# Second mixer of an encoder trunk: queries and keys projected with features on the partitions, rotated by block swaps, values projected apart

## The chip, the cores and the metric

The kernel runs on one core of one Trainium2 chip. The metric is the device time of one execution, in microseconds (us). The core has a matrix engine (TensorE, PE), a vector engine (VectorE, DVE), an activation engine (ScalarE, ACT), GpSimd (POOL) and a queue engine (SyncE, SP). Each works through its own instructions in order, and DMAs are issued from the queues of SP, POOL or ACT. SBUF is the on-chip memory with 128 partitions, PSUM the memory that TensorE writes.

## What is computed

The reference is a trunk of two layers over two groups of requests, one sequence of 256 tokens and one of 512, with 1024 features. Each layer is a token mixer and a feed-forward part, both between RMS norms. The change is in the second mixer, differential attention:

```python
def diff_attention(h, w_in, w_o, lq1, lk1, lq2, lk2, subln_g, lambda_init):
    b, s, _ = h.shape
    qkv = h @ w_in
    q, k, v = jnp.split(qkv, [B_QK_DIM, 2 * B_QK_DIM], axis=-1)
    q = q.reshape(b, s, 2 * B_HEADS, HEAD_DIM)
    k = k.reshape(b, s, 2 * B_HEADS, HEAD_DIM)
    v = v.reshape(b, s, B_HEADS, 2 * HEAD_DIM)
    cos, sin = rope_tables(s, HEAD_DIM)
    q = (apply_rope(q, cos, sin) * (HEAD_DIM ** -0.5)).reshape(b, s, B_HEADS, 2, HEAD_DIM)
    k = apply_rope(k, cos, sin).reshape(b, s, B_HEADS, 2, HEAD_DIM)
...
        sc = jnp.einsum('bqhcd,bkhcd->bhcqk', qi, k).astype(jnp.float32)
        p = jax.nn.softmax(sc, axis=-1)
        a = p[:, :, 0] - lam * p[:, :, 1]
        return jnp.einsum('bhqk,bkhe->bqhe', a.astype(v.dtype), v)
...
    o = rms_norm(o, subln_g) * (1.0 - lambda_init)
    return o.reshape(b, s, B_V_DIM) @ w_o
```

There are 8 heads. A head has two halves (c above) of 64 features each for queries and keys, and one value of 128. `apply_rope` splits 64 features into two blocks of 32, and each block needs the other one: x1·cos − x2·sin and x2·cos + x1·sin.

## The kernel before, in words

**Tiling.** The 768 tokens are 6 tiles of 128 (t = 0 to 5): tiles 0 and 1 are the sequence of 256, tiles 2 to 5 that of 512. Everything is float32. A product is made of three matmuls of a rounded type (F32R): each operand is the sum of a high and a low part (`hi`, `lo`), and `product_steps` (L315 to L317) adds hi·hi, hi·lo and lo·hi. With 1024 features in 8 blocks of 128, a product is 24 matmuls. `h_hi` and `h_lo` hold the normed tokens with features on the partitions, in two halves of three tiles.

**Weights.** SP loads weights in blocks (`wraw`), ACT casts the high part (L222) and DVE subtracts it for the low part (L223), ahead of their use, into a ring of buffers. `take` gets the next block, `free` lets the ring go on.

**The units of the second mixer.** `mixer_b` runs 48 units, head by head and tile by tile. A unit (`unit`) multiplies one tile of tokens (the stationary operand) with 384 columns of weights (the moving one): q, k and v of one head, into a PSUM bank `pqb`, with tokens on the partitions. Its `end` copies v (L787), rotates q and k on DVE (`rope`, L530 to L536; there the two blocks lie in the free dimension), and splits them into high and low parts `bsp` (L794 to L798). Scores need features on the partitions. So two units later, after four steps of the products, `turn` runs: three transposes of k on TensorE into `tkb` (L808), two of q into `tqb` (L810), an ACT copy to `kb` (L811) and a DVE copy to `qb` (L812).

**Attention.** For each head and tile there are three steps. `score`: four matmuls into two banks `bsc` (L828, L831), the row maximum (L834), a tiny negation (L835), exponentials with their sum on ACT (L837), and the combination of both halves on DVE (`rden`, `rho`, `be`: L842 to L847). `turn_e`: transposes of the probabilities into `tpa` (L859) and a copy `aT` on ACT (L861). `values`: matmuls into `pob` (L871), an ACT copy into `ob` (L875) and the sum of squares (L877). From head 6 on, POOL scales a row's heads by the sub-norm: `rstd_sub` (L360, its first step on ACT in L359), then `ob` times it (L884): heads 0 to 6 at head 6, head 7 at head 7.

**Order.** The program is written in the order in which these pieces are called, and each engine takes its own in an order close to it. `plan` and `last_plan` say after which step of a unit's products a piece of attention is called; one call of `advance` is the score of a tile, the transposes of the tile two calls before and the values of the tile three calls before. After the units comes the out projection of 2 × 6 units (`po`, 512 columns each); its operands are transposes of `ob` into `tp_o` (L407), with ACT and DVE making high and low parts (L414, L415). The list `run` interleaves its first three units with the last pieces of attention by hand. `gains(2)`, two vectors of 1024 spread over the partitions (`gpost`, `gpre`), is loaded ahead of the mixer and used by the out projection. The pool `xpool` has two buffers with the tag "x" of 4 KB a partition.

Of the kernel before, what the change touches and what calls it, by code (L numbers as in the profile page):

```python
# [46 lines left out]
def trunk(  # L47
# [7 lines left out]
    wb,  # L55
    wo,
# [6 lines left out]
    sin,  # L63
    yp,
# [113 lines left out]
    for h in range(8):  # L178
        for i in range(4):
            plain(wb[h, i], 768)  # L180
# [584 lines left out]
    def mixer_b(gp, g_next, first_steps, o):  # L765
        with ExitStack() as st:
            ap = st.enter_context(tc.tile_pool(name="bpool", bufs=1, side="right", reuse_waits="tile"))
            ssh = [ap.tile([P, 8], F32, name=f"ssh{t}") for t in range(NT)]
            kk, vv, q, wk = {}, {}, {}, {}
            pending = {}  # L770

            def unit(i):

                h, t = divmod(i, NT)
                first, n = seq_of(t)
                if t == 0:
                    wk[h] = column_blocks(take(4), HALF)
                    free(4)
                pm = bank(f"pqb_{i}")
                steps = product_steps(pm[:, :HALF], [(htile(t, k), wk[h][k]) for k in range(KT)])  # L780
                if t == NT - 1:
                    steps = releasing(steps, 4)

                def end():
                    if t == first:
                        vv[h, first] = ap.tile([P, n, P], F32, tag=f"v{first}", name=f"vb{h}_{first}", bufs=2)
                    nc.scalar.copy(out=vv[h, first][:, t - first], in_=pm[:, 256:384])  # L787
                    qk = ap.tile([P, 4, HD], F32, tag="qk", name=f"bqk{i}", bufs=2)
                    rope(ap, qk, pm[:, :256].rearrange("p (n d) -> p n d", d=HD), 4, t, f"b{i}")

                    sp = ap.tile([P, 5, 2, HD], F32R, tag="sp", name=f"bsp{i}", bufs=2)
                    s4 = sp.rearrange("p a b d -> p (a b) d")
                    k2 = qk[:, 2:4].rearrange("p c (o d) -> p c o d", o=1).broadcast_to([P, 2, 2, HD])
                    nc.scalar.copy(out=s4[:, 0:4:3], in_=qk[:, 0:2])  # L794
                    nc.scalar.copy(out=sp[:, 2:4], in_=k2)
                    nc.vector.tensor_tensor(
                        out=s4[:, 1:3], in0=qk[:, 0:2], in1=s4.bitcast(F32)[:, 0:4:3], op=ALU.subtract)
                    nc.vector.tensor_tensor(  # L798
                        out=sp[:, 4], in0=qk[:, 2:4], in1=sp.bitcast(F32)[:, 2:4, 0], op=ALU.subtract)

                    def turn():
                        if t == first:
                            kk[h, first] = ap.tile([P, 3, n * P], F32R, tag=f"k{first}", name=f"kb{h}_{first}")
                        q[i] = ap.tile([P, 2, P], F32R, tag="q", name=f"qb{i}", bufs=5)
                        tq, tk = ps.tile([P, 512], F32R, tag="ps", name=f"tqb{i}"), ps.tile([P, 512], F32R, tag="ps", name=f"tkb{i}")
                        at = slice((t - first) * P, (t - first + 1) * P)
                        for j in range(3):
                            nc.tensor.transpose(tk[:, j * P:(j + 1) * P], sp[:, 2 + j].rearrange("p a d -> p (a d)"), ident_r)  # L808
                        for j in range(2):
                            nc.tensor.transpose(tq[:, j * P:(j + 1) * P], sp[:, j].rearrange("p a d -> p (a d)"), ident_r)  # L810
                        nc.scalar.copy(out=kk[h, first][:, :, at], in_=tk.bitcast(F32)[:, :3 * P].rearrange("p (k n) -> p k n", k=3))  # L811
                        nc.vector.tensor_copy(out=q[i].rearrange("p h n -> p (h n)"), in_=tq.bitcast(F32)[:, :256])  # L812

                    pending[i] = turn

                return steps + [end]
# [3 lines left out]
            def score(i):  # L820
                h, t = divmod(i, NT)
                first, n = seq_of(t)
                den = small.tile([P, 2], F32, tag="den", name=f"bden{i}")
# [3 lines left out]
                for c in range(2):  # L827
                    nc.tensor.matmul(ss[c], q[i][:, c], kk[h, first][:, c], start=True, stop=False)  # L828

                for c, rows in enumerate((slice(0, HD), slice(HD, P))):  # L830
                    nc.tensor.matmul(ss[c], q[i][rows, c], kk[h, first][rows, 2], start=False, stop=True)  # L831
                for c, s in enumerate(ss):
                    mx = small.tile([P, 1], F32, tag="mx", name=f"bmx{i}_{c}")
                    nc.vector.tensor_reduce(out=mx, in_=s, axis=AX.X, op=ALU.max)  # L834
                    nc.vector.tensor_scalar(out=mx, in0=mx, scalar1=-HD ** -0.5, scalar2=None, op0=ALU.mult)  # L835
                    e = e2[:, c * 512:c * 512 + 512]
                    nc.scalar.activation(  # L837
# [25 lines left out]

            def values(i):
                h, t = divmod(i, NT)
                first, n = seq_of(t)
                _, rden = blocks.pop(i)
                aT = aTs.pop(i)
                po = bank(f"pob{i}")
# [35 lines left out]
            for i in range(8 * NT):  # L905
# [16 lines left out]
                for s in placed(att, at, fill):  # L922
                    s()
# [555 lines left out]
```

## Time and profile before

| what | value |
|---|---|
| median of three runs | 1689.34 us (1686.83, 1689.34, 1690.02) |
| span of the profiled execution, first to last instruction | 1686.6 us |
| profiled execution's own time | not listed apart; its span lies 0.2 us under the fastest run |
| mean granted TensorE clock | 0.997 |
| first and last start of a product of the second mixer (`pqb`) | 790.3 and 1106.6 us |
| DVE, ACT, POOL busy, of the span | 74%, 56%, 5% |
| moved by DMAs | 207.30 MB, 123 GB/s on average |

The profile lists busy time by engine. TensorE's matmuls are pipelined: a listed duration overlaps the next one, so a matmul's price in a full queue is the distance from its start to the next start. A row of groups reads: line, engine, operation, out<-in, shapes, count, then busy us and mean ns, then the idle time ahead of them and what ended it. Three numbers with slashes are the shortest, median and longest duration in ns.

### The profile page before, as it was taken

Reading aid. Unit: us, or ns where it says so; the run is one execution under the profiler, and the core shown is the slowest. Engines: PE = TensorE matmul, PEld = TensorE weight load, DVE = VectorE, ACT = ScalarE, POOL = GpSimd, SP = SyncE. Lnnn points to the kernel's source line nnn. Section 1 sums busy time; section 2 is a strip of 40 time slices with the busy share of each in tenths; the row PEclk is TensorE's granted clock in tenths of the full one; section 3 lists DMA queues with packets and bytes.
Section 4 is the critical chain, followed back from the end, with each engine's and each line's share of the span. In section 5 each row is a group of like instructions: output and inputs, shape, how many; then the busy total and the mean of one; then the engine's idle time right before and its main releaser. Section 6 shows DMA issues by size and latency. Waiting matters only on the chain. (4 is left out here: it accounts for less than half of the span.)

```text
span 1686.6 us, 25513 instructions
## 1 busy us (share of the span) xinstructions
PE 1659.1 (98%) x9483; PEld 1514.3 (90%) x9483; DVE 1251.3 (74%) x2488; ACT 949.7 (56%) x2158; POOL 81.7 (5%) x104
## 2 busy tenths in 40 slices
PE   7999999999999999999999999999899999999998
PEld 7888878899999998888999999988799999998887
DVE  7888766896766666988777676874997666666886
ACT  6777775654444444556566666674744444444553
POOL 1000001000000000001000000331000000000001
PEclk9999999999999999999999999999999999999999
DMA  6111014534333347666211111113444343336765
GB/s 212 39 38 48 14 38 150 175 134 140 109 125 99 128 139 250 230 235 205 83 39 38 38 38 38 48 51 113 170 138 141 108 141 108 128 114 226 249 222 176
DMA packets 62107, 207.30 MB, mean 123 GB/s; under 512 B 6752, under 2 KB 8928, under 8 KB 61728
## 3 DMA queue, kind: packets, MB, share of 16 engines
q1 hardware_dynamic: 55152, 175.15, 30.8%
q0 software_dynamic: 6688, 30.28, 5.6%
q8 instruction: 74, 1.21, 0.3%
q14 instruction: 49, 0.40, 0.1%
q10 hardware_dynamic: 144, 0.26, 0.0%
HBM read 162.80 MB, written 42.86 MB: 122 GB/s over the span
## 5 line engine op out<-in xcount | busy, mean ns | idle before, releaser
L223 DVE TENSOR_TENSOR wlo<-wraw,whi 128x1024 fp32r<-128x1024 f32 (+2 forms) x180 | 204.9, 1144 | 173.9 <-ACT whi L222 172.7
L222 ACT CAST whi<-wraw 128x1024 fp32r<-128x1024 f32 (+2 forms) x180 | 176.5, 986 | 117.4 <-PE py L316 58.9
L315 PE MATMUL py<-hhi,whi 128*128 128x384 f32 x464 | 155.4, 335 | 0.8 <-ACT u L976 0.8
L317 PE MATMUL py<-hhi,wlo 128*128 128x384 f32 x464 | 155.0, 334 | 0.0
L316 PE MATMUL py<-hlo,whi 128*128 128x384 f32 x464 | 155.0, 334 | 0.0
L315 PE MATMUL pqb<-whi,hhi 128*128 128x384 f32 x384 | 136.5, 356 | 0.0
L316 PE MATMUL pqb<-wlo,hhi 128*128 128x384 f32 x384 | 128.9, 336 | 0.0
L317 PE MATMUL pqb<-whi,hlo 128*128 128x384 f32 x384 | 128.8, 335 | 0.0
L303 ACT CAST hhi<-araw 128x768 fp32r<-128x768 f32 (+1 forms) x74 | 57.6, 783 | 94.6 <-DMA araw<-act 94.2
L317 PE MATMUL pv<-whi,hlo 128*128 128x512 f32 (+1 forms) x240 | 92.2, 384 | 0.4 <-DVE hlo L304 0.4
L315 PE MATMUL pv<-whi,hhi 128*128 128x512 f32 (+1 forms) x240 | 92.4, 385 | 0.0
L316 PE MATMUL pv<-wlo,hhi 128*128 128x512 f32 (+1 forms) x240 | 92.1, 384 | 0.0
L304 DVE TENSOR_TENSOR hlo<-araw,hhi 128x768 fp32r<-128x768 f32 (+1 forms) x74 | 65.2, 889 | 32.3 <-ACT hhi L303 32.1
L315 PEld LDWEIGHTS py<-hhi,whi 128*128 128x128 f32 x464 | 87.1, 188 | 1.7 <-ACT u L976 1.4
L316 PEld LDWEIGHTS py<-hlo,whi 128*128 128x128 f32 x464 | 87.1, 188 | 0.0
L317 PEld LDWEIGHTS py<-hhi,wlo 128*128 128x128 f32 x464 | 87.1, 188 | 0.0
L315 PE MATMUL po<-whi,hhi 128*128 128x512 f32 x192 | 77.9, 406 | 0.2 <-ACT hhi L303 0.2
L317 PE MATMUL po<-whi,hlo 128*128 128x512 f32 x192 | 75.4, 393 | 0.2 <-DVE hlo L304 0.2
L316 PE MATMUL po<-wlo,hhi 128*128 128x512 f32 x192 | 75.3, 392 | 0.0
L315 PEld LDWEIGHTS pqb<-whi,hhi 128*128 128x128 f32 x384 | 72.3, 188 | 2.0 <-issue 1.7
L315 PE MATMUL pqa<-whi,hhi 128*128 128x384 f32 x192 | 73.9, 385 | 0.0
L315 PE MATMUL px<-hhi,whi 128*128 128x384 f32 x208 | 70.8, 342 | 2.7 <-ACT hhi L303 2.7
(303 smaller groups left out, 4829.6 us busy)
## 6 DMA issues: line engine op xcount, KB each, us to landing
act<-st POOLq DMA_DIRECT2D x22, 1344.0 KB, 6.6
wraw<-in_wgu SPq DMA_DIRECT2D x56, 512.0 KB, 4.6
araw<-act SPq DMA_DIRECT2D x70, 384.0 KB, 4.0
y_wraw<-in_wgu SPq DMA_DIRECT2D x40, 512.0 KB, 3.6
wraw<-in_wd SPq DMA_DIRECT2D x40, 512.0 KB, 3.9
wraw<-in_wb SPq DMA_DIRECT2D x32, 384.0 KB, 3.2
xd<-x SPq DMA_DIRECT2D x18, 512.0 KB, 3.0
x<-xd SPq DMA_DIRECT2D x18, 512.0 KB, 4.1
```

The source lines that it names most:

```text
L222: state["raw_hi"] = nc.scalar.copy(out=hi, in_=src)
L223: state["raw_lo"] = nc.vector.tensor_tensor(out=lo, in0=src, in1=hi.bitcast(F32), op=ALU.subtract)
L303: state["hi"] = nc.scalar.copy(out=hi, in_=src)
L304: state["lo"] = nc.vector.tensor_tensor(out=lo, in0=src, in1=hi.bitcast(F32), op=ALU.subtract)
L315: nc.tensor.matmul(out, ah, bh, start=start and i == 0, stop=False, skip_group_check=more)
L316: nc.tensor.matmul(out, ah, bl, start=False, stop=False, skip_group_check=more)
L317: nc.tensor.matmul(out, al, bh, start=False, stop=stop and i == last, skip_group_check=more)
```

## The change

Queries and keys are no longer projected tile by tile. `rotated` makes a unit of one head's q or k for one half of the tokens (three tiles): the weights are the stationary operand and 384 tokens the moving one, so the result (`pqb` or `pkb`) has features on the partitions, as scores need them. The two blocks of 32 features that rotation combines now lie on different partitions. ACT copies the result to `x` (L834, with the scaling of q), four DMAs from POOL's queue write it with neighbouring blocks of 32 partitions swapped (L836), and DVE multiplies the copy (L838) and the swapped one (L839) with tables `rope_b` and adds them (L840). ACT casts the two halves of 64 features (L849). For q, DVE subtracts the high from the full values into the other half's partitions (L852). For k, two more DMAs from POOL's queue copy the high parts there (L855), and DVE makes the low parts (L856). There are 32 such units. Values are projected apart by `straight`, for groups of 2, 3 and 3 heads and tile by tile, 18 units. `b_fill` is the order of these 50 units.

The tables take the buffers of `gpost` and `gpre`, and the gains are loaded after the units. Pieces of attention stand at positions in a list `events`, counted in units; `run` is written anew and holds two score tiles of head 6 and all six of head 7, with three out-projection banks open at once. The sub-norm is applied at heads 3, 6 and 7 (heads 0 to 3, 4 to 6, and 7). The negation of the row maximum is done by the maximum itself, and the exponential no longer scales. Line numbers in this section are those of the changed program.

```diff
+def b_fill():
+
+    qk = lambda hs, halves, kinds: [(kind, h, i) for i in halves for h in hs for kind in kinds]
+    v = lambda g: [("v", g, t) for t in range(NT)]
+    out = qk((0,), (0,), "qk") + v(0) + qk((0,), (1,), "qk")
+    for h in range(1, 8):
+        out += qk((h,), (0, 1), "qk") if h == 7 else qk((h,), (0, 1), "q") + qk((h,), (0, 1), "k")
+        if h in (2, 5):
+            out += v(h // 2)
+    return out
...
+        if kind == "v":
+            for i in range(4 if V_HEADS[n] == 3 else 2):
+                w = 2 * HALF if V_HEADS[n] == 3 else D
+                plain(wbv[n, i, :, :w], w)
+        else:
+            plain(wb[n, "qk".index(kind)], D)
...
+            tab = []
+            for i, tag in enumerate(("gpost", "gpre")):
+                full = gpool.tile([P, D], F32, tag=tag, name=f"rope{i}")
+                nc.sync.dma_start(out=full[:, :2 * HALF], in_=rope_b[i])
+                tab.append(full[:, :2 * HALF].rearrange("p (h n) -> p h n", h=2))
...
+            def rotated(kind, h, half):
+
+                (whi, wlo), = held((kind, h), 1)
+                bk = bank(f"p{kind}b{h}_{half}")
+                pm = bk[:, :HALF]
+                steps = product_steps(pm, [
+                    (tuple(w[:, k * P:(k + 1) * P] for w in (whi, wlo)), (h_hi[half][:, k], h_lo[half][:, k]))
+                    for k in range(KT)])
...
+                def end():
+                    x = xpool.tile([P, 2, HALF], F32, tag="x", name=f"x{kind}{h}_{half}")
+                    s, r = x[:, 0], x[:, 1]
+                    nc.scalar.activation(out=s, in_=pm, func=AF.Copy, scale=HD ** -0.5 if kind == "q" else 1.0)
+                    for a in range(4):
+                        nc.gpsimd.dma_start(out=r[a * 32:a * 32 + 32], in_=s[(a ^ 1) * 32:(a ^ 1) * 32 + 32])
+                    z = ap.tile([P, HALF], F32, tag="z", name=f"z{kind}{h}_{half}", bufs=2)
+                    nc.vector.tensor_tensor(out=z, in0=s, in1=tab[0][:, half], op=ALU.mult)
+                    nc.vector.tensor_tensor(out=r, in0=r, in1=tab[1][:, half], op=ALU.mult)
+                    nc.vector.tensor_tensor(out=z, in0=z, in1=r, op=ALU.add)
+                    if kind == "q":
+                        d = q[h, half] = ap.tile([P, 2, HALF], F32R, tag="q", name=f"qb{h}_{half}", bufs=4)
+                        homes = (d[:, 0], d[:, 1])
+                    else:
+                        if half == 0:
+                            kk[h] = ap.tile([P, 3, 2 * HALF], F32R, tag="k", name=f"kb{h}", bufs=2)
+                        homes = (kk[h][:, 0, cols], kk[h][:, 1, cols])
+                    for rows, b in zip((up, down), homes):
+                        nc.scalar.copy(out=b[rows], in_=z[rows])
+                    if kind == "q":
+                        for rows, other, b in zip((up, down), (down, up), homes):
+                            nc.vector.tensor_tensor(out=b[other], in0=z[rows], in1=b[rows].bitcast(F32), op=ALU.subtract)
+                    else:
+                        for rows, other, b in zip((up, down), (down, up), homes):
+                            nc.gpsimd.dma_start(out=b[other], in_=b[rows])
+                            nc.vector.tensor_tensor(
+                                out=kk[h][rows, 2, cols], in0=z[rows], in1=b[rows].bitcast(F32), op=ALU.subtract)
+
...
+            def straight(g, t):
+                n = V_HEADS[g] * P
+                taken = held(("v", g), 4 if n == HALF else 2)
+                wide = [tuple(w[:, j * n:(j + 1) * n] for w in u) for u in taken for j in range(KT // len(taken))]
+                pm = bank(f"pvb{g}_{t}")[:, :n]
+                steps = product_steps(pm, [(htile(t, k), wide[k]) for k in range(KT)])
...
+                    vv[g, t] = ap.tile([P, n], F32, tag="v", name=f"vb{g}_{t}", bufs=9)
+                    nc.scalar.copy(out=vv[g, t], in_=pm)
...
                     mx = small.tile([P, 1], F32, tag="mx", name=f"bmx{i}_{c}")
-                    nc.vector.tensor_reduce(out=mx, in_=s, axis=AX.X, op=ALU.max)
-                    nc.vector.tensor_scalar(out=mx, in0=mx, scalar1=-HD ** -0.5, scalar2=None, op0=ALU.mult)
+                    nc.vector.tensor_reduce(out=mx, in_=s, axis=AX.X, op=ALU.max, negate=True)
                     e = e2[:, c * 512:c * 512 + 512]
-                    nc.scalar.activation(
-                        out=e[:, :n * P], in_=s, func=AF.Exp, bias=mx, scale=HD ** -0.5,
-                        accum_out=den[:, c:c + 1])
+                    nc.scalar.activation(out=e[:, :n * P], in_=s, func=AF.Exp, bias=mx, accum_out=den[:, c:c + 1])
...
-                if h >= 6:
-
-                    hs = slice(0, 7) if h == 6 else slice(7, 8)
+                if h in (3, 6, 7):
+
+                    hs = {3: slice(0, 4), 6: slice(4, 7), 7: slice(7, 8)}[h]
...
+            events = []
+
+            def spread(h, start, stop):
+                for t in range(NT):
+                    events.append((start + (stop - start) * t / NT, "s", h * NT + t))
+
+            for h, start, stop in (
+                    (0, 12, 16.7), (1, 16.7, 22.2), (2, 22.2, 28.8), (3, 29.6, 34.8), (4, 34.8, 40.3), (5, 40.3, 46)):
+                spread(h, start, stop)
+            events += [(47.9 + t / 2, "s", 6 * NT + t) for t in range(4)]
+            for n in range(2, len(events)):
+                events.append((events[n][0], "t", n - 2))
+            for n in range(3, 6 * NT + 4):
+                events.append((events[n][0], "v", n - 3))
+            kinds = {"s": score, "t": turn_e, "v": values}
+            events.sort(key=lambda e: e[0])
+
...
+            gp, g_next = gains()
...
+            run = S(6, 4) + early[0] + T(6, 2) + V(6, 1) + early[1] + out[0][:2] + S(6, 5) + T(6, 3) + V(6, 2) + out[0][2:4]
+            run += S(7, 0) + early[2] + T(6, 4) + V(6, 3) + out[1][:2] + S(7, 1) + T(6, 5) + V(6, 4) + out[1][2:4] + early[3]
+            run += S(7, 2) + T(7, 0) + V(6, 5) + out[2][:2] + S(7, 3) + T(7, 1) + V(7, 0) + out[2][2:4] + early[4]
+            run += S(7, 4) + T(7, 2) + V(7, 1) + late[0] + early[5] + out[0][4:6] + S(7, 5) + T(7, 3) + V(7, 2) + late[1]
+            run += out[0][6:] + T(7, 4) + V(7, 3) + late[2] + out[1][4:6] + T(7, 5) + V(7, 4) + out[1][6:] + late[3]
+            run += out[2][4:6] + V(7, 5) + out[2][6:]
```

The removed lines that are left out are in the functions shown above. The host lays out the weights anew (`wb` by head and kind with 1024 columns, `wbv` by group) and makes the tables `rope_b`.

**TensorE, between two score tiles.** In the names of before, `pqb_15` is the product of unit 15, `tkb13` and `tqb13` the transposes of unit 13, `bsc11` a score of unit 11. Before:

```order
L317 MATMUL pqb_15_9688<-whi141_9340,hlo1_114 128x384
L808 MATMUL tkb13_9703<-ident_r_86,bsp13_9584 128x128 x3
L810 MATMUL tqb13_9702<-ident_r_86,bsp13_9584 128x128 x2
L315 MATMUL pqb_15_9688<-whi142_9398,hhi1_112 128x384
L316 MATMUL pqb_15_9688<-wlo142_9399,hhi1_112 128x384
L317 MATMUL pqb_15_9688<-whi142_9398,hlo1_114 128x384
L828 MATMUL bsc11_0_9716<-kb1_2_9261,qb11_9527 128x512
L828 MATMUL bsc11_1_9717<-kb1_2_9261,qb11_9527 128x512
L831 MATMUL bsc11_0_9716<-kb1_2_9261,qb11_9527 128x512
L831 MATMUL bsc11_1_9717<-kb1_2_9261,qb11_9527 128x512
L859 MATMUL tpa9_9735<-ident_81,be9_9600 128x128 x4
```

Now, where the first score of head 3 (`bsc18`) follows q of head 4 (`pqb4_1`, its second half of the tokens):

```order
L347 MATMUL pqb4_1_10237<-hlo1_114,whi146_9862 128x384
L348 MATMUL pqb4_1_10237<-hhi1_112,wlo146_9863 128x384
L890 MATMUL bsc18_0_10258<-kb3_10109,qb3_0_9961 128x256
L890 MATMUL bsc18_1_10259<-kb3_10109,qb3_0_9961 128x256
L893 MATMUL bsc18_0_10258<-kb3_10109,qb3_0_9961 128x256
L893 MATMUL bsc18_1_10259<-kb3_10109,qb3_0_9961 128x256
L918 MATMUL tpa16_10275<-ident_81,be16_10059 128x128 x4
L931 MATMUL pob15_10282<-vb1_2_9685,aT15_10159 128x128
```

The transposes of k and q are gone; the scores read `kb3` and `qb3_0`, which DVE, ACT and POOL's DMAs have written.

**DVE, in the third head before and at k of the fourth head now.** Before (`bqk18` is the rotated q and k of unit 18, `be14` the probabilities of unit 14):

```order
L796 TENSOR_TENSOR bsp18_10033<-bqk18_10026,bsp18_10033 128x128
L798 TENSOR_TENSOR bsp18_10033<-bqk18_10026,bsp18_10033 128x128
L812 CAST qb17_10051<-tqb17_10052 128x256
L834 TENSOR_REDUCE bmx14_0_10075<-bsc14_0_10069 128x1
L834 TENSOR_REDUCE bmx14_1_10079<-bsc14_1_10070 128x1
L835 TENSOR_SCALAR bmx14_0_10075<-bmx14_0_10075 128x1
L835 TENSOR_SCALAR bmx14_1_10079<-bmx14_1_10079 128x1
L842 RECIPROCAL rden14_10083<-bden14_10067 128x2
L530 TENSOR_TENSOR r1_b19_10102<-pqb_19_10038,cos_sb_100 128x256
L844 SCALAR_TENSOR_TENSOR rho14_10085<-rden14_10083,bden14_10067,nlam_110 128x1
L532 TENSOR_TENSOR r2_b19_10103<-pqb_19_10038,sin_sb_101 128x4x32
L847 SCALAR_TENSOR_TENSOR be14_10068<-be14_10068,rho14_10085 128x512
```

Now (`xk3_0` is the copy and its swapped form, `zk3_0` the rotated half of k):

```order
L839 TENSOR_TENSOR xq3_1_10027<-xq3_1_10027,rope1_8534 128x384
L838 TENSOR_TENSOR zk3_0_10105<-xk3_0_10099,rope0_8532 128x384
L840 TENSOR_TENSOR zq3_1_10033<-zq3_1_10033,xq3_1_10027 128x384
L852 TENSOR_TENSOR qb3_1_10037<-zq3_1_10033,qb3_1_10037 64x384 x2
L896 TENSOR_REDUCE bmx17_0_10143<-bsc17_0_10137 128x1
L896 TENSOR_REDUCE bmx17_1_10146<-bsc17_1_10138 128x1
L839 TENSOR_TENSOR xk3_0_10099<-xk3_0_10099,rope1_8534 128x384
L840 TENSOR_TENSOR zk3_0_10105<-zk3_0_10105,xk3_0_10099 128x384
L901 RECIPROCAL rden17_10149<-bden17_10135 128x2
L903 SCALAR_TENSOR_TENSOR rho17_10151<-rden17_10149,bden17_10135,nlam_110 128x1
L906 SCALAR_TENSOR_TENSOR be17_10136<-be17_10136,rho17_10151 128x512
L856 TENSOR_TENSOR kb3_10109<-zk3_0_10105,kb3_10109 64x384 x2
```

A row of L839 waits for four DMAs, and the softmax rows of tile 17 (`rden17` to `be17`) stand behind the one of `xk3_0`.

**POOL, before and after the last units.** Before, POOL has no DMA in the mixer, and only the sub-norm rows (`rstd_sub`, `ob`). Now:

```order
L836 DMA xq7_0_11545<-xq7_0_11545 32x384 x4
L855 DMA kb6_11432<-kb6_11432 64x384 x2
L836 DMA xk7_0_11619<-xk7_0_11619 32x384 x4
L855 DMA kb7_11629<-kb7_11629 64x384 x2
L836 DMA xq7_1_11733<-xq7_1_11733 32x384 x4
L391 TENSOR_TENSOR rstd_sub36_11788<-rstd_sub36_11788,mhalf_102 128x3
L944 TENSOR_TENSOR ob0_8517<-ob0_8517,rstd_sub36_11788 128x384
L836 DMA xk7_1_11813<-xk7_1_11813 32x384 x4
L391 TENSOR_TENSOR rstd_sub37_11875<-rstd_sub37_11875,mhalf_102 128x3
L944 TENSOR_TENSOR ob1_8518<-ob1_8518,rstd_sub37_11875 128x384
L855 DMA kb7_11629<-kb7_11629 64x384 x2
L391 TENSOR_TENSOR rstd_sub38_11926<-rstd_sub38_11926,mhalf_102 128x3
```

The swaps of one unit stand between the swaps and the copies of k of another, and from `rstd_sub36` (head 6) on, between sub-norm rows.

More of the change, by code (lines that the diff above doesn't have):

```diff
@@ L177, in trunk @@
     ffn_units(0)
-    for h in range(8):
-        for i in range(4):
-            plain(wb[h, i], 768)
+    seen = set()
+    for kind, n, _ in b_fill():
+        if (kind, n) in seen:
+            continue
+        seen.add((kind, n))
+        if kind == "v":
[4 more added lines that the diff above has]
+            plain(wb[n, "qk".index(kind)], D)
     for n2 in range(2):
@@ L784, in end @@
                 def end():
[L785 to L812, printed above, removed]
@@ new lines, in mixer_b @@
+            for n in range(3, 6 * NT + 4):
+                events.append((events[n][0], "v", n - 3))
+            kinds = {"s": score, "t": turn_e, "v": values}
+            events.sort(key=lambda e: e[0])
+            for i, (kind, n, j) in enumerate(b_fill()):
+                fill = straight(n, j) if kind == "v" else rotated(kind, n, j)
+                fill = first_steps.pop(i, []) + fill
+                now = [(at, f, m) for at, f, m in events if i <= at < i + 1]
+                att = [lambda f=f, m=m: kinds[f](m) for _, f, m in now]
+                for s in placed(att, [int((at - i) * len(fill)) for at, _, _ in now], fill):
@@ L1406, in trunk @@
     o, ostack = rows("ob")
-    later = mixer_b(*gains(2), later, o)
+    later = mixer_b(lambda: gains(2), later, o)
     later, *held = later
@@ L1430, in _layout @@
     w = f("b_w_in")[0]
-    q, k, v = (w[:, i * 1024:(i + 1) * 1024].reshape(D, 8, 128) for i in range(3))
-    out["wb"] = groups(np.concatenate([q, k, v], axis=2), 8)
+    q, k, v = (w[:, i * 1024:(i + 1) * 1024] for i in range(3))
+    blocks = lambda m: m.reshape(KT, P, 8, P).transpose(2, 1, 0, 3).reshape(8, P, D)
+    out["wb"] = c(np.stack([blocks(q), blocks(k)], axis=1))
+    out["wbv"] = np.zeros((3, 4, P, D), np.float32)
+    at = 0
+    for g, n in enumerate(V_HEADS):
+        cols = v[:, at:at + n * P]
+        at += n * P
+        m, per = (4, 2) if n == 3 else (2, 4)
+        out["wbv"][g, :m, :, :per * n * P] = cols.reshape(m, per, P, n * P).transpose(0, 2, 1, 3).reshape(m, P, per * n * P)
     def halves(w):
@@ L1456, in _layout @@
     out["sin"] = tab(np.concatenate([-sn, sn], axis=1))
+    rows = lambda a: np.concatenate([a[:256], a]).T
+    out["rope_b"] = c(np.stack([np.tile(rows(np.concatenate(p, axis=1)), (2, 1)) for p in ((cs, cs), (-sn, sn))]))
     return out
```

91 lines of the change are left out of this document (37 added, 54 removed).

## The prediction

> **What bounds the kernel now.** I read the page's first part, then the mixer in stretches of 50 us, then what TensorE waits for there. Times are us from the start of the span.
>
> ```profile
> PE 1659.1 (98%) x9483; PEld 1514.3 (90%) x9483; DVE 1251.3 (74%) x2488; ACT 949.7 (56%) x2158; POOL 81.7 (5%) x104
> ```
> ```profile
> core 0: us, PE busy (x) PEld busy (x) DVE busy (x) ACT busy (x) POOL busy (x), PEclk, DMA share, GB/s
> 900.00:950.00 50.00, 50.00 (x327) 46.64 (x325) 35.62 (x106) 31.77 (x96) 0.00 (x0) 1.00 0.19 56
> 950.00:1000.00 50.00, 50.00 (x316) 45.33 (x314) 34.78 (x110) 30.27 (x93) 0.00 (x0) 1.00 0.11 33
> 1050.00:1100.00 50.00, 50.00 (x334) 46.19 (x333) 38.70 (x112) 34.01 (x110) 15.82 (x10) 1.00 0.13 41
> 1100.00:1150.00 50.00, 49.05 (x273) 39.81 (x272) 29.98 (x60) 29.87 (x79) 10.82 (x15) 1.00 0.14 43
> ```
> ```profile
> PE tp_o L407 <- POOL ob L884: 0.6, 1, 0.6
> PE pob L871 <- ACT aT L861: 0.2, 1, 0.2
> ```
>
> TensorE (PE) is busy in all 50.00 of 50 us of the mixer, at a granted clock of 1.00, and the last two rows are all its waits from the first `pqb` (790.3) to the second half of the out projection (1154.5). This stretch is a queue of TensorE instructions. What leaves the queue is saved in full, and a new wait is paid in full. DVE has about 36 of 50 us, ACT 31: room, but not so much that any chain through them is free.
>
> **What leaves TensorE.** 48 units each end in three transposes of k and two of q:
>
> ```profile
> L808 PE MATMUL tkb<-ident_r,bsp x144: 222/229/304, 807.3 to 1113.6; 128*128 128x128 f32 x144
> L810 PE MATMUL tqb<-ident_r,bsp x96: 243/249/256, 807.5 to 1113.7; 128*128 128x128 f32 x96
> ```
>
> Those durations overlap, since matmuls are pipelined; the price is the distance between starts:
>
> ```profile
> start us, us, engine line op out<-in xcount [idle before <-releaser]
> 869.07 0.33 PE L316 MATMUL pqb<-wlo,hhi 128*128 128x384 f32 x1
> 869.24 0.34 PE L317 MATMUL pqb<-whi,hlo 128*128 128x384 f32 x1
> 869.41 0.37 PE L808 MATMUL tkb<-ident_r,bsp 128*128 128x128 f32 x3
> 869.62 0.34 PE L810 MATMUL tqb<-ident_r,bsp 128*128 128x128 f32 x2
> 869.80 0.41 PE L315 MATMUL pqb<-whi,hhi 128*128 128x384 f32 x1
> 870.05 0.33 PE L316 MATMUL pqb<-wlo,hhi 128*128 128x384 f32 x1
> 870.91 0.63 PE L828 MATMUL bsc<-kb,qb 128*128 128x512 f32 x2
> 871.47 0.50 PE L831 MATMUL bsc<-kb,qb 64*128 64x512 f32 x2
> 871.89 0.38 PE L871 MATMUL pob<-vb,aT 128*128 128x128 f32 x1
> ```
>
> The five take 869.80 − 869.41 = 0.39, so 48 × 0.39 = **18.7** leave. The next `pqb` takes 0.25 to the one after it, where a step is otherwise 0.17: each turn costs 0.08 more for breaking the run of products. I count 40 of the 48, since the others stand beside attention and that break remains: **3.2**.
>
> **What is added on TensorE.** q and k: before, 48 × 24 products of 384 columns did q, k and v. Now 32 units for q and k and 12 for v do 44 × 24 of them, and 6 units for v do 24 of 256 columns: 96 fewer at 0.17 (−16.3), 144 more at the step of 256 columns:
>
> ```profile
> 43.33 0.28 PE L630 MATMUL sc<-kha,qa 128*128 128x256 f32 x1
> 43.45 0.28 PE L631 MATMUL sc<-kla,qa 128*128 128x256 f32 x1
> ```
>
> 0.12 each, +17.3: together **+1.0**. Scores, transposes of the probabilities and value products keep their number and shapes. TensorE's queue is thus 18.7 + 3.2 − 1.0 = **20.9 shorter**. That the transposes were hidden anyway is excluded by the 50.00 rows: they stand in the queue, not beside it.
>
> **DVE and ACT, in sum.** A DVE operation of 256 columns takes 0.424 and of 128 columns 0.281, so I estimate 384 columns at 0.57:
>
> ```profile
> L530 DVE TENSOR_TENSOR r_b<-pqb,cos_sb x48: 404/424/426, 801.8 to 1108.0; 128x256 f32<-128x256 f32 x48
> L532 DVE TENSOR_TENSOR r_b<-pqb,sin_sb x48: 271/281/287, 802.2 to 1108.3; 128x128 f32<-128x128 f32 x48
> L812 DVE CAST qb<-tqb x48: 405/418/425, 808.9 to 1114.0; 128x256 fp32r<-128x256 f32 x48
> ```
>
> Removed per unit: two of 256, four of 128 columns, and the copy of `tqb`: 2.39, × 48 = 115. Added per rotated unit: two multiplies, an add and two subtractions, 5 × 0.57 = 2.85, × 32 = 91. DVE had about 36/50 of 364 us = 262; it will have 238 of 343, or 69%. The small negations (L835) go too. ACT loses casts and copies and gains none that outweigh them. On average neither becomes the bound. What counts is where they are late.
>
> **The new chain.** A half of k must now pass: ACT copy, four swap DMAs issued on POOL's queue, landing, multiply and add on DVE, two casts on ACT, two more POOL DMAs, landing. The rows:
>
> ```profile
> L811 ACT CAST kb<-tkb 128x384 fp32r<-128x384 f32 x32 | 15.2, 476 | 17.3 <-PE tkb L808 17.0
> ```
> ```profile
> L1029 POOL DMA_DIRECT2D act<-st x22 | 19.4, 881 | 635.8 <-DVE st L1028 607.3 <-DVE wraw L261 28.6
> ```
> ```profile
> act<-st POOLq DMA_DIRECT2D x22, 1344.0 KB, 6.6
> araw<-act SPq DMA_DIRECT2D x14, 192.0 KB, 3.5
> ys<-x SPq DMA_DIRECT2D x1, 256.0 KB, 2.1
> gpost<-in_g_post SPq DMA_DIRECT2D x4, 512.0 KB, 5.0
> ```
>
> The trace shows no DMA inside SBUF and none of 48 KB. Its issue lies between nothing and the 0.88 of POOL's only kind of DMA; its landing between nothing and 6.6. I take 0.88, the only POOL row, and 2.1, the smallest landing, since 48 KB is nearest to it. The chain: 0.48 + 4 × 0.88 + 2.1 + 2 × 0.57 + 2 × 0.48 + 2 × 0.88 + 2.1 = **12.1 us**. The time it has is shortest at head 3. Behind the last product of k's half 0 stand 66 products (66 × 0.17 = 11.2), and the scores, transposes and values of one tile. By the last rows of the timeline the scores take 871.89 − 870.91 = 0.98; four transposes and eight passes of values I estimate at 0.11 each, 1.3. In all **13.5 us**. So it just fits. In units of the fill order, from the end of k's half 0 to the head's first score, heads 1 to 6 have 3.7, 5.2, 2.6, 3.8, 5.3 and 2.9; a unit is 24 × 0.17 = 4.1 and the attention within it, so only heads 3 and 6 are near the chain, and head 7, whose last unit ends where its scores begin to be wanted. Any queue ahead of it on POOL or DVE makes it late. On POOL the swaps of the next q stand between k's swaps and k's halves; on DVE the second multiply (L839) holds back all that stands behind it, softmax work included, until the swap has landed. I charge 1 us at each of heads 3, 6 and 7: **+3** (bounds 0, and the 10 of the second rival).
>
> **The tail.** The six last score tiles and the transposes of heads 6 and 7 now stand inside three out-projection units. TensorE has there 72 products of 512 columns (estimate 0.17 × 512/384 = 0.23, 16.6), six tiles at 0.98 and two shorter at 0.7, and 36 + 40 transposes and 2 × 38 passes of values at 0.11: about **40.6 us**. ACT in the same piece, by these rows:
>
> ```profile
> L837 ACT ACTIVATE be<-bsc,bmx 128x512 f32<-128x512 f32 x48 | 32.6, 683 | 8.1 <-DVE bmx L835 8.1
> L837 ACT ACTIVATION_READ_ACCUMULATOR be<-bsc,bmx 128x1 f32 x69 | 13.6, 196 | 0.0
> L861 ACT COPY aT<-tpa 128x512 f32<-128x512 f32 x24 | 14.1, 586 | 12.0 <-PE tpa L859 12.0
> L875 ACT ACTIVATE ob<-pob,rden 128x128 f32<-128x128 f32 x37 | 13.6, 368 | 20.3 <-PE pob L871 20.2
> L877 ACT ACTIVATE sq<-ob 128x128 f32<-128x128 f32 x37 | 11.5, 312 | 0.9
> L414 ACT ACTIVATE hhi<-tp_o,subl 128x512 fp32r<-128x512 f32 x12 | 8.2, 682 | 0.8 <-PE tp_o L407 0.8
> ```
>
> Twelve exponentials of 512 columns with their accumulator reads, 12 × 0.88 = 10.5; four shorter, 2.7; eight copies `aT` and two shorter, 5.4; eleven `ob` 4.0 and `sq` with its read 5.6; nine `hhi`, 6.1; eleven small `rstd_sub`, 3.2; three evacuations, two biases and two casts, about 4: **41.5 us**. That equals TensorE's time, where the same engine had 29.87 of 50 in the last stretch quoted above. Two engines that are both full and wait for each other do not overlap wholly; I charge a tenth, **+4** (bounds 0 and 8).
>
> **What else moves.** The weights of q, k and v hold as many bytes as before, in 26 blocks for 32, so SP's loads and their splitting on ACT and DVE cost what they did. The two gains are loaded behind the units and land after 5.0; the first that needs them is the end of an out-projection unit, over 20 us later. Part of the scaling of heads moves from heads 6 and 7 to head 3: on POOL, no more columns than before, six more `rstd_sub`, and between the swaps. I charge these nothing; what is left over of their cover is in the term of the chain.
>
> **The sum.** −20.9 + 3 + 4 = −13.9. The profiled span is 1686.6, and the fastest run shown is 1686.83, so almost nothing lies around it; the median is 1689.3. From the median: 1689.3 − 13.9 = **1675.4**, given as 1675. At the start of the mixer I charge nothing: no attention stands in its first twelve units, so nothing waits there for a chain.
>
> **The rivals.**
>
> *All covers hold.* No chain is late and ACT keeps up: 1689.3 − 20.9 = **1668**. For it: 69% on DVE, and four heads with over 3.5 units. Against it: 12.1 of 13.5, 41.5 of 40.6.
>
> *The chain is late at each head.* If a swap lands after 3.5, as the 192 KB row does, the chain is 14.9 and misses head 3 by 1.4; each of 32 multiplies then also holds DVE about 3 us longer than the row before it covers, so softmax is late in heads 1 to 5 as well. About 1.5 at each of seven heads in place of my 3 in all: +7.5, or **1683**, and up to 1689. The two `x` buffers work the same way: a third rotated unit's copy (L834) waits for the first unit's add, and behind that copy wait ACT's exponentials.
>
> *The DMAs go one after another.* Twenty per head, and heads 3 to 5 have twelve rotated units in a row, so 60 DMAs. Per head TensorE has four units (16.3), four large tiles (2.3 each) and two small: 28.5 us, 85 in three heads. At x us per DMA POOL's queue falls behind by 60x − 85, of which some 10 are slack. It eats the forecast's 14 where 60x = 109, at **x = 1.8**; at 2.1, a landing each, it loses 60 × 2.1 − 95 = 31 and gives **1706**. For it: one operation on POOL took 1.54 beside a DVE subtraction of two SBUF tiles, and 0.55 later:
>
> ```profile
> 1102.35 2.29 DVE L223 TENSOR_TENSOR wlo<-wraw,whi 128x1024 fp32r<-128x1024 f32 x1 [0.83 <-ACT whi L222]
> ...
> 1103.52 1.54 POOL L360 TENSOR_TENSOR rstd_sub<-rstd_sub,mhalf 128x1 f32<-128x1 f32 x1
> 1126.45 0.55 POOL L360 TENSOR_TENSOR rstd_sub<-rstd_sub,mhalf 128x1 f32<-128x1 f32 x1 [19.42 <-ACT rstd_sub L359]
> ```
>
> Against it: 0.88 is already a mean of issues beside a busy DVE, and 1.8 is twice that. [...]
>
> **How the numbers follow.** Forecast 1675 (1671 to 1680): 0.43. All covers hold, 1668: 0.18. Late at each head, 1681 to 1689: 0.25, of which 0.14 below 1686. One after another, from 1689 up, 1706: 0.14. Measurement can tell about 0.2%, 3.4 us, from no change. Faster by more: 0.43 + 0.18 + 0.14 = 0.75; within: 0.10; slower: 0.15. The range runs from 1666, below the case with no wait, to 1692, which takes in the late chain and leaves out most of the last rival.
>
> **What would show it.** Each step has its trace: `tkb` and `tqb` gone; the stretch from the first q product to the second half of the out projection at 343 plus its waits; waits of TensorE's scores for DVE or ACT at heads 3, 6 and 7 of about 1 each, and about 4 in all in the tail, for ACT. Rival two shows as DVE idle before L839 and scores waiting at heads 1, 2, 4 and 5. Rival three shows as POOL's DMA issues over 1.8 apart while their copies are long done. The forecast is wrong if issue plus landing of a swap is far from 5.6 us in all, or if ACT's queue in the tail is not what TensorE waits for.

## The result, and the profile after

The changed kernel takes **1679.5 us** (median of five, 1678.2 to 1684.0) against 1689.3 before. The ratio is 0.9947, with a 95% interval of 0.9934 to 0.9960. The forecast was 1675, in a range of 1666 to 1692. In the profiled executions the stretch from the first product of the second mixer to the second half of the out projection went from 364.4 us (790.3 to 1154.7) to 353.9 (788.6 to 1142.5): 10.5 less, where the prediction had 13.9. That 10.5 is a difference of two larger numbers, as the runs below show.

The page's first part, then the mixer in stretches of 50 us, as before (engine busy times, granted clock, DMA share):

```profile
PE 1638.5 (98%) x9291; PEld 1495.1 (89%) x9291; DVE 1235.2 (74%) x2210; ACT 943.9 (56%) x2080; POOL 162.5 (10%) x276
```
```profile
core 0: us, PE busy (x) PEld busy (x) DVE busy (x) ACT busy (x) POOL busy (x), PEclk, DMA share, GB/s
900.00:950.00 50.00, 49.75 (x305) 46.31 (x305) 32.56 (x62) 29.00 (x76) 11.88 (x24) 1.00 0.30 84
950.00:1000.00 50.00, 48.83 (x296) 44.02 (x294) 39.46 (x76) 31.69 (x93) 29.41 (x46) 1.00 0.31 80
1000.00:1050.00 50.00, 47.07 (x280) 43.34 (x281) 31.77 (x61) 31.82 (x85) 7.42 (x15) 0.97 0.23 69
1050.00:1100.00 50.00, 45.34 (x268) 39.21 (x268) 38.49 (x81) 34.97 (x100) 22.16 (x37) 0.97 0.40 110
```

TensorE, which had 50.00 in every one of these stretches, now has gaps, and in two of them the clock column is no longer 1.00. No other engine is full in any of these stretches, so the gaps are not the sign of an engine that is busy throughout. TensorE's waits in the mixer (us in total, times, longest):

```profile
PE tpa L918 <- ACT aT L920: 4.1, 1, 4.1
PE po L346 <- ACT hhi L445: 2.9, 1, 2.9
PE pob L931 <- ACT aT L920: 1.2, 2, 1.0
PE tpa L918 <- DVE be L906: 0.7, 2, 0.4
PE tp_o L438 <- ACT aT L920: 0.3, 1, 0.3
```

Before, they were 0.6 and 0.2. Each of these rows names ACT or DVE, never a DMA; the DMA stands further back. The timeline of the first one (start, duration, engine, what; rows of TensorE's products and of other work left out):

```profile
988.74 0.50 POOL L836 DMA_DIRECT2D xk<-xk  x1 [0.36 <-ACT xk L834]
...
991.03 1.05 ACT L849 CAST kb<-zk 64x384 fp32r<-64x384 f32 x2 [2.58 <-DVE zk L840]
991.84 1.05 POOL L855 DMA_DIRECT2D kb<-kb  x2 [2.61 <-ACT kb L849]
...
992.90 1.16 POOL L391 TENSOR_TENSOR rstd_sub<-rstd_sub,mhalf 128x4 f32<-128x4 f32 x1
...
994.03 0.56 POOL L836 DMA_DIRECT2D xk<-xk  x1
994.62 1.05 POOL L944 TENSOR_TENSOR ob<-ob,rstd_sub 128x512 f32<-128x512 f32 x1
995.61 0.55 POOL L836 DMA_DIRECT2D xk<-xk  x1
...
997.73 0.50 POOL L836 DMA_DIRECT2D xk<-xk  x1 [1.57 <-issue]
...
999.49 1.32 DVE L839 TENSOR_TENSOR xk<-xk,rope 128x384 f32<-128x384 f32 x1 [2.44 <-DMA xk<-xk]
1000.84 0.56 DVE L840 TENSOR_TENSOR zk<-zk,xk 128x384 f32<-128x384 f32 x1
1001.43 1.04 ACT L849 CAST kb<-zk 64x384 fp32r<-64x384 f32 x2 [4.77 <-DVE zk L840]
...
1002.50 0.37 ACT L920 COPY aT<-tpa 128x256 f32<-128x256 f32 x1
...
1002.93 1.00 PE L918 MATMUL tpa<-ident,be 128*128 128x128 f32 x4 [4.10 <-ACT aT L920]
```

These are the swaps of the last half of k of head 5. Between the first (988.74) and the fourth (997.73) lie 9.0 us, where four issues in a row take 1.5 from first to last start. What stands between them on POOL's queue is the copies of the half of k ahead, which wait 2.61 for ACT's cast, and two rows of the sub-norm of head 3. By these rows the 9.0 are 1.6 of issuing swaps, 3.7 of the two copies with their wait, 2.1 of the sub-norm rows, and 1.6 in which the profile shows nothing to wait for. DVE waits for the last swap, ACT's cast waits for DVE, the copy `aT` of an attention tile that has nothing to do with this k stands behind the cast, and TensorE waits for `aT`.

### The profile page after: what moved, and what is told of

It is laid out like the page before. It is cut to its first block, busy times and chain, and to the rows that moved or that the text cites. A ratio compares the mean times of both kernels' runs of the same rounds, so it can differ in the third digit from the quotient of the medians.

```text
span 1676.5 us, 25190 instructions
## 1 busy us (share of the span) xinstructions
PE 1638.5 (98%) x9291; PEld 1495.1 (89%) x9291; DVE 1235.2 (74%) x2210; ACT 943.9 (56%) x2080; POOL 162.5 (10%) x276
## 5 line engine op out<-in xcount | busy, mean ns | idle before, releaser
L1082 POOL DMA_DIRECT2D act<-st x22 | 19.4, 882 | 635.9 <-DVE st L1081 635.9
L898 ACT ACTIVATE be<-bsc,bmx 128x512 f32<-128x512 f32 (+1 forms) x96 | 58.5, 614 | 24.6 <-DVE bmx L896 24.3
L347 PE MATMUL px<-hlo,whi 128*128 128x384 f32 x208 | 70.0, 337 | 1.2 <-DVE hlo L335 1.2
L391 POOL TENSOR_TENSOR rstd_post<-rstd_post,mhalf 128x1 f32<-128x1 f32 x23 | 16.4, 716 | 557.9 <-ACT rstd_post L390 557.9
```

What stands on the lines that cost most here:

```text
L347: nc.tensor.matmul(out, ah, bl, start=False, stop=False, skip_group_check=more)
L391: nc.gpsimd.tensor_tensor(out=r[:, :w], in0=r[:, :w], in1=mhalf[:, :w], op=ALU.pow)
L898: nc.scalar.activation(out=e[:, :n * P], in_=s, func=AF.Exp, bias=mx, accum_out=den[:, c:c + 1])
L1082: nc.gpsimd.dma_start(out=at_hand[c // 4][:, :, c // 2 % 2], in_=out.pop(c // 2))
```

## The experiments

Each time is compared with the kernel before, run beside it on the same chip. "Stretch" is the one defined above, from the first product of the second mixer to the second half of the out projection, in each profiled execution. An edit also changes the order in which the engines take their instructions, and in some runs (e8 and e9) that matters as much as the edit itself.

| run | median us | ratio (95%) | stretch |
|---|---|---|---|
| before | 1688.9 to 1689.9 | 1 | 364.4 |
| changed | 1679.5 | 0.9947 (0.9934 to 0.9960) | 353.9 |
| e1 sub-norm late | 1689.4 | 1.0000 (0.9989 to 1.0011) | 364.1 |
| e2 no swaps | 1666.9 | 0.9857 (0.9840 to 0.9875) | 342.1 |
| e3 swaps on ACT's queue | 1679.8 | 0.9941 (0.9924 to 0.9959) | 356.2 |
| e4 swaps on SP's queue | 1667.2 | 0.9864 (0.9842 to 0.9885) | 344.6 |
| e5 copies of k on SP's queue | 1677.3 | 0.9933 (0.9918 to 0.9948) | 351.0 |
| e6 before, two transposes of five | 1677.4 | 0.9938 (0.9923 to 0.9953) | 352.9 |
| e7 swaps and copies on SP's queue | 1670.4 | 0.9898 (0.9870 to 0.9925) | 343.7 |
| e8 each swap twice | 1692.2 | 1.0019 (1.0003 to 1.0035) | 363.6 |
| e9 swaps of head 5 on SP's queue | 1675.2 | 0.9912 (0.9898 to 0.9926) | 347.5 |
| e10 swaps of head 7 on SP's queue | 1676.4 | 0.9918 (0.9905 to 0.9931) | 349.0 |
| e11 changed, again | 1680.1 | 0.9942 (0.9927 to 0.9957) | 354.5 |
| e12 as e4, again | 1670.9 | 0.9887 (0.9872 to 0.9902) | 343.9 |

**e6: what the transposes cost.** In the kernel before:

```diff
-                        for j in range(3):
+                        for j in range(1):
...
-                        for j in range(2):
+                        for j in range(1):
...
```

> The kernel before, with one transpose of k and one of q in each turn in place of three and two (the copies read the one block three times and twice, so scores are not computed rightly). It leaves out 144 of 240 transposes. If they stand in TensorE's queue as the prediction says, 144 x 0.39/5 = 11.2 us go: 1678. If they were hidden beside other work, 1687 or more.

The stretch got 364.4 − 352.9 = 11.5 shorter, the time 11.5. That is 0.080 for each transpose, and 19.3 for all 240 if the others cost the same. TensorE's waits in the stretch grew from 0.8 to 1.8, so without waits it is 12.5, or 0.087 each and 20.8 for all. The transposes stood in the queue, as the prediction had it (18.7).

**e1: the sub-norm away from the swaps.**

```diff
-                if h in (3, 6, 7):
+                if h in (6, 7):
...
-                    hs = {3: slice(0, 4), 6: slice(4, 7), 7: slice(7, 8)}[h]
+                    hs = {6: slice(0, 7), 7: slice(7, 8)}[h]
```

> The sub-norm of heads 0 to 3 goes back to head 6 (one scaling of 0 to 6, as before), so no POOL scaling stands between the swaps of heads 4 and 5. Theory A (the 4.1 us wait near 998 comes from swaps held behind the sub-norm on POOL's queue, passed on in order through DVE's second multiply and ACT's cast to the copies of the probabilities): that wait falls under 1, the half clock behind it goes too, the tail gets at most 1.5 longer by POOL's scaling of seven heads; time about 1675. Theory B (issue and landing of the swaps alone make the chain late): the wait near 998 stays above 3; time 1679 to 1681.

The wait near 998 is gone, and the products up to the last one of k took 281.8 us instead of 288.5 (first to last start). But the tail lost far more than the 1.5 expected, and the time is 1689.4 where about 1675 was expected. The reason is in one row of TensorE's waits, and the granted clock is 0.50 for 24 us around them:

```profile
PE tp_o L438 <- POOL ob L944: 16.1, 3, 7.2
```

I had not moved the early transposes of heads 0 to 3 in `run`. With the sub-norm at head 6 they wait for head 6's values and POOL's scaling. So e1 says nothing about the tail as it is. Near 998 it shows that the wait goes with the sub-norm: the four swaps start within 4.3 us, ACT takes cast and `aT` in the same order as before, and both come earlier. What went is more than the two rows: the swaps of the half ahead are no longer held apart either, so the copies of k are issued before the first swap and not between the swaps. And DVE's second multiply, which takes 1.32 beside the next sub-norm scaling on POOL (999.36 to 1000.39), takes 0.56.

**e2: no swaps.**

```diff
-                    for a in range(4):
-                        nc.gpsimd.dma_start(out=r[a * 32:a * 32 + 32], in_=s[(a ^ 1) * 32:(a ^ 1) * 32 + 32])
...
-                    nc.vector.tensor_tensor(out=r, in0=r, in1=tab[1][:, half], op=ALU.mult)
+                    nc.vector.tensor_tensor(out=r, in0=s, in1=tab[1][:, half], op=ALU.mult)
```

> Leaves out the 128 swap DMAs: the second multiply reads the copy itself, so rotation is not computed; all engine work stays. Theories A and B both: the waits near 998 and 1064 go, and the cast of q that ACT holds ahead of the out projection is no longer late, so the wait of 2.9 at the first out-projection product shrinks under 1; time 1668 to 1671. Theory C (ACT simply has too much work in the tail, swaps or not): the waits from 1064 on keep 4 to 6 us; time 1673 to 1675.

1666.9, a little under what was expected, and the waits left in the stretch are 0.7, 0.3 and 0.2:

```profile
PE po L346 <- ACT hhi L445: 0.7, 1, 0.7
PE tp_o L438 <- ACT aT L918: 0.3, 1, 0.3
PE tpa L916 <- ACT be L896: 0.2, 1, 0.2
```

ACT's work in the tail is the same here, and TensorE hardly waits for it (1.2 in the stretch). Theory C, a full ACT, falls.

**e4 and e12, e3: the swaps on other queues.** One word is changed: `nc.gpsimd.dma_start` of the swaps becomes `nc.sync.dma_start` (e4, e12) or `nc.scalar.dma_start` (e3).

> The 128 swaps are issued from SP's queue, between its weight loads. Theory A: the wait near 998 goes unless a swap stands behind a load that waits for its buffer; 1672 to 1676 if none does, 1680 or more if loads hold swaps back by more than 4 us, which shows as DVE waiting longer before the second multiply than the 2.4 us of now. Theory B: no change in that wait with the same landing time; 1678 to 1681.

> All swaps on SP's queue, once more, beside the changed kernel: 1665 to 1669, so 11 to 14 below it. If head 5 and head 7 are all of it, its gain over the changed kernel is the sum of theirs within 3 us.

> The 128 swaps are issued from ACT's queue right behind the copy instead of POOL's. Theory A: the swaps no longer stand behind the sub-norm, the wait near 998 falls under 1; but every issue now stands in ACT's own order. If an issue costs ACT under 0.1 us: 1673 to 1676. If it costs ACT what it costs POOL (0.5 us), 64 us more on ACT, the tail grows by 5 or more: 1680 to 1690. Theory B: no gain near 998 either way.

On SP's queue the time is 1667.2, five under the expected span, and 1670.9 in e12, two over the span expected there. Beside the latter the changed kernel took 1680.1, so 9.2 us are gained, less than the 11 to 14 expected. The stretch of e12 is 343.9, within 2 us of the kernel with no swaps at all. The swap itself is no faster there (e4):

```profile
xq<-xq SPq DMA_DIRECT2D x64, 48.0 KB, 2.0
xk<-xk SPq DMA_DIRECT2D x64, 48.0 KB, 2.0
```

On POOL's queue the same rows show 2.0 and 1.8. From ACT's copy to the last of the four landings the median of the 32 units is 5.0 in e12 and 4.9 in the changed kernel; head 5's last half of k takes 4.9 in place of 11.0. So the gain lies where something stood between the swaps. In e12, that half is swapped in one go:

```profile
992.33 0.33 SPq L227 DMA_DIRECT2D wraw<-in_wb  x1
992.98 2.42 SPq L836 DMA_DIRECT2D xk<-xk  x4
```

On ACT's queue (e3) the wait near 998 is gone as well, but each issue takes 0.5 to 0.6 of ACT's order. In the tail, head 7's issues, 0.51, 0.60 and twice 0.6, stand ahead of exponentials and `hhi`, and TensorE waits there for 6.5. Gain and loss cancel: 1679.8, just under the span that was expected where an issue costs ACT 0.5.

**e5 and e7: the copies of k on SP's queue**, alone and with the swaps (in `b[other]` and `b[rows]` read as float32):

```diff
-                            nc.gpsimd.dma_start(out=b[other], in_=b[rows])
+                            nc.sync.dma_start(out=b[other].bitcast(F32), in_=b[rows].bitcast(F32))
```

> Only the 32 copies of k's high parts move from POOL's queue to SP's; the swaps stay on POOL with the sub-norm of head 3 among them. Theory A (the sub-norm between the swaps): the wait of 4.1 near 998 stays above 3, time 1677 to 1681. Theory D (the copies of k, which wait for ACT's casts at the head of POOL's queue, hold the swaps back): the wait falls under 1, time 1672 or less.

> Swaps and copies of k all on SP's queue. Theory A: as with the swaps alone on SP, 1665 to 1669, since what stood between the swaps is gone already. Theory D: 2 us or more lower than that. If a waiting copy holds SP's weight loads, the tail grows and the time is 1671 or more.

e5 lies between the two theories: the wait near 998 fell from 4.1 to 1.5, neither above 3 nor under 1. The four swaps of that half of k start within 6.3 us, where the changed kernel needs 9.0 and e1 4.3. The two gains, 2.7 here and 4.7 in e1, do not add up to shares of the 9.0: in e1 the copies moved as well, and in e5 the sub-norm row between the swaps now waits 2.70 for ACT itself. Both kinds of row hold the swaps apart; how much each does alone was not measured. The interval of e5's time overlaps that of the changed kernel; part of what was gained near 998 is lost at the first out-projection product, where the wait grew from 2.9 to 3.8. e7 (1670.4, its executions from 1665.8 to 1677.3) lies between the 1669 and the 1671 that were expected, and its interval overlaps that of e4: no gain of the copies of k shows beyond that of the swaps.

**e8: each swap twice.**

```diff
-                    for a in range(4):
+                    for a in (0, 1, 2, 3, 0, 1, 2, 3):
```

> Each swap is issued twice on POOL, which makes every chain longer by four issues of 0.5, 2 us, and POOL's queue fuller by 64 us. Theory A with chains near their limit: waits at heads 3, 5, 6 and 7, time 1684 to 1692. If chains away from the sub-norm have slack of over 2 us (theory A, with slack): only the two waits that exist grow, by 2 each, time 1681 to 1684.

12.7 us slower than the changed kernel (1692.2), at the slow end of what was expected. A new kind of wait appears, for the copies of k themselves, once at head 3 (941) and once at head 6 (1060):

```profile
PE bsc L890 <- DMA kb<-kb: 5.8, 2, 3.6
```

These are two of the three heads that the prediction counted as near their limit (3, 6 and 7); at heads 1, 2, 4 and 5 no score waits. The expectation priced the edit too low, though. From the last product of k's first half to the landing of its copies, the trace shows 16.3 us at head 3 and 18.7 at head 6, against 10.7 and 11.1 in the changed kernel: 5.5 and 7.5 more and not 2, since the doubled swaps of other units stand in the same queue (at head 3, those of q from 927.1 to 930.7). In the changed kernel these copies land 2.9 and 3.6 us before the first scores of heads 3 and 6, so both heads fit there with that much to spare.

The wait near 998 is gone in e8, although head 5's last swaps land no earlier after their product than in the changed kernel (16.4 us against 15.8). ACT's order is another one there: the same `aT` stands ahead of the late cast, and nothing on TensorE waits for that cast.

```profile
1001.70 0.35 ACT L920 COPY aT<-tpa 128x256 f32<-128x256 f32 x1
...
1006.68 1.05 ACT L849 CAST kb<-zk 64x384 fp32r<-64x384 f32 x2 [2.62 <-DVE zk L840]
```

So the wait needs both, swaps held apart and an `aT` behind the cast.

**e9 and e10: swaps on SP's queue for head 5 or head 7 alone.**

```diff
-                        nc.gpsimd.dma_start(out=r[a * 32:a * 32 + 32], in_=s[(a ^ 1) * 32:(a ^ 1) * 32 + 32])
+                        (nc.sync if h == 5 else nc.gpsimd).dma_start(out=r[a * 32:a * 32 + 32], in_=s[(a ^ 1) * 32:(a ^ 1) * 32 + 32])
```

> Swaps from SP's queue for head 5 alone (16 of 128); all others stay on POOL. If the loss ahead of the out projection comes from the swaps of head 5's k, held apart on POOL's queue by the sub-norm and by the copies of k, the wait near 998 and the half clock behind it go: the stretch from the first q product to the last product of k gets 5 to 7 us shorter, the time is 1672 to 1674, and the tail keeps its 6 us of waits. If the loss is spread over all heads: 1677 to 1679.

> Swaps from SP's queue for head 7 alone. If the waits of the tail come from head 7's swaps on POOL's queue (behind sub-norm rows of head 6), the wait of 2.9 at the first out-projection product falls to about 1.7, as with all swaps on SP, with no half clock behind it, and the time is 1675 to 1677, with the wait near 998 kept. If ACT's queue is simply full there: tail and time as in the changed kernel, 1679 to 1680.

Beside the changed kernel (1680.1), head 5 alone gives 4.9 and head 7 alone 3.7; together 8.6 of the 9.2 that all heads give. In e9 the wait near 998 is gone and the 2.9 at the out projection stays, with waits for `be` in the tail grown to 1.9. ACT's order has changed there as well (`aT` at 996.85, the cast at 1001.06), so e9 alone would not show that the swaps are the cause; in e12 the cast stands ahead of `aT` as in the changed kernel, and there is no wait. The stretch of e9 is 7.0 shorter than in e11 and the time only 4.9, 1.2 over the expected span; the stretch starts 1.8 later, for a reason that stays open. In e10 the waits are the other way round: 2.6 near 998, and 1.5 at the out projection, with no half clock behind it. Its time is in the expected span, but its interval overlaps that of e11, so this gain rests on the trace.

**e11** (the changed kernel again):

> The changed kernel itself, beside the three others on the same chip: 1678 to 1681.

It did.

## Why the prediction was right

- **What leaves TensorE's queue: −20.9, measured about −22.7.** The stretch without its waits is 342.1 − 1.2 = 340.9 in e2, and 343.9 − 3.0 = 340.9 in e12; before it is 364.4 − 0.8 = 363.6. The transposes are 19.3 to 20.8 of it by e6, so the breaks in the run of products and the narrower values give 1.9 to 3.4 together, where I had 3.2 − 1.0 = 2.2. These two were not measured apart.
- **The chain at heads 3, 6 and 7: +3, measured nothing at the scores of any head.** Where I charged it, the chain was shorter than the 12.1 that I worked out (10.7 and 11.1 for the first halves of heads 3 and 6), and the cover at head 3 was 13.7, as estimated: the copies land 2.9 and 3.6 ahead of the scores. Over the 16 halves of k the chain took 10.3 to 21.5. An issue on POOL took 0.51 and not the 0.88 of the only row before, and a landing 1.8 to 2.0, near the 2.1 that I took. The sign that I gave for being wrong, issue plus landing of a swap far from 5.6 us in all, shows only at head 5: from copy to last landing it is 3.5 in the quickest units, 4.9 in the median one and 11.0 there.

```profile
L836 POOL DMA_DIRECT2D xk<-xk x64 | 31.9, 505 | 30.7 <-ACT xk L834 18.6 <-ACT rstd_sub L390 4.7 <-ACT sq L937 2.3
xq<-xq POOLq DMA_DIRECT2D x64, 48.0 KB, 2.0
xk<-xk POOLq DMA_DIRECT2D x64, 48.0 KB, 1.8
```

- **What was late instead.** "Any queue ahead of it on POOL or DVE makes it late" was the right mechanism, put at the wrong place. I counted slack from k to its own score. The wait arose at head 5, whose k had 5.3 units, because the late cast held back an unrelated tile's `aT` on ACT. The step that failed is the charge for the sub-norm among the swaps, priced at nothing, and with it the copies of k, whose wait for ACT's cast I had not counted against the swaps behind them: of the 9.0 us between first and fourth swap, 2.1 are sub-norm rows and 3.7 the copies with their wait. Without the sub-norm (e1) the swaps lie 4.3 apart and the wait is gone. That this wait of 4.1 is near my +3 is luck.
- **The tail: +4 for a full ACT, measured 4.9, for another reason.** The rows of ACT sum to what TensorE needs there, but e2 shows that TensorE would wait only 1.2 for it. With head 7's swaps on SP's queue (e10) 3.3 of the 4.9 are left and the half clock behind them is gone; the 2.1 between 3.3 and 1.2 were not taken apart. The cast of q waits for DVE and the swap, and `hhi`, which TensorE waits for, stands behind it:

```profile
1079.81 1.04 ACT L849 CAST qb<-zq 64x384 fp32r<-64x384 f32 x2 [1.34 <-DVE zq L840]
...
1082.40 0.68 ACT L445 ACTIVATE hhi<-tp_o,subl 128x512 fp32r<-128x512 f32 x1
```

- **What no step held: half the clock.** After each of the two long waits the granted clock is 0.50 for 3.41 us, which costs 3.4 us in all (last section).

So the changed kernel's stretch is 340.9, plus the 9.2 of waits quoted above, plus 3.4 for the clock: 353.5, measured 353.9. Every other run made from the changed kernel gives 340.2 to 342.1 for its stretch without waits and the loss at half clock. The gain was larger than forecast by 2 and the losses by 6 (12.6 for 7). Signs and order of size were right, the errors partly cancel, and the sum came out 3.4 us off in the stretch and 4 in the time.

**The rivals.** *All covers hold* (1668) is close to e2 (1666.9) and to e4 and e12 (1667.2 and 1670.9), and the change is not there. *The chain is late at each head* (1683) named rightly that DVE's second multiply is late and that ACT's later work stands behind the chain, but it is one head and the tail, not all, and ACT's row is the cast L849 and not the copy L834. *The DMAs go one after another* (1706) falls: four swaps, issued 0.5 apart, have all landed 3.5 us after the copy in the quickest units and 4.9 in the median one, where four landings in a row would be 8. Yet a queue in order does set the pace: with four more issues in each unit, e8 went to the slow side (1692.2).

## What to carry to other kernels

Where TensorE is the bound, as here, a DMA that swaps partitions can replace transposes (1689.3 us became 1679.5), but its queue is part of the chain: put it on a queue where nothing that waits stands between its pieces. Here that is SP's, and one word gains another 9.2 us (e12 against e11, with no interval of overlap: 0.9872 to 0.9902 against 0.9927 to 0.9957). When slack is counted, count it for everything that stands behind the waiting instruction on each engine that the chain passes, not only for the result of the chain.

## What the runs showed of the hardware

A wait of TensorE cost more than its length here. The stretches of 2 us around the first wait (granted clock third from the end):

```profile
1000.00:1002.00 2.00, 0.00 (x0) 0.00 (x0) 1.97 (x4) 0.54 (x2) 0.40 (x1) 1.00 0.00 0
1002.00:1004.00 2.00, 1.07 (x5) 0.88 (x6) 1.78 (x4) 1.92 (x6) 1.12 (x2) 0.77 0.27 49
1004.00:1006.00 2.00, 2.00 (x8) 2.00 (x9) 0.86 (x3) 1.89 (x6) 0.00 (x0) 0.50 0.28 49
1006.00:1008.00 2.00, 2.00 (x11) 2.00 (x11) 1.47 (x3) 1.09 (x3) 0.00 (x0) 0.87 0.00 0
1008.00:1010.00 2.00, 2.00 (x13) 1.60 (x11) 1.14 (x3) 1.38 (x6) 0.00 (x0) 1.00 0.03 8
```

The busy columns say 2.00 of 2 while TensorE does half the work: products of 384 columns start 0.32 apart at 1005 and 0.18 apart at 1007. In windows of 0.02 us, the clock of the changed kernel is 0.50 for 3.41 us from 1003.10 and again for 3.41 us from 1085.02, and 1.00 in the rest of the mixer. In windows of 4 us, the half clock adds up to 17.0 and 6.8 us in e1 and to 13.7 in e3, which is five, two and four times as long. Work for 3.41 us at half clock loses 1.7; the changed kernel has two such pieces in the mixer, 3.4 us. They begin 0.17 us after the end of the wait of 4.1 and 1.90 after the end of the wait of 2.9. Single waits of 2.2 (e8) and 2.6 (e10) were followed by half clock as well, but not every wait was: the 2.9 of e9's tail was followed by none, the same wait in e11 by 6.83 us of it, and a single wait of 2.0 (e12) by none. In e8 a piece begins at 1088.8, within a wait of 1.4 that follows one of 0.7 by less than 2 us. What starts a piece was not shown. So the wait of 2.9 ahead of the out projection cost about 3 in e9, 5 here and 6 in e11, and part of the scatter between executions of such a kernel may come from there; that was not tested.

What released the fourth swap at 997.73, 1.57 us after the profile shows nothing more to wait for, stays open. It is there without the sub-norm as well (2.79 in e1, where the swap starts 0.08 after the second copy of k has landed), and absent in e5, where the copies of k are issued elsewhere.
